# Weight parts of whole projections beside each other, element by element, in one tile

## The chip, the cores and the metric

One core of one Trainium2 chip runs the kernel. The metric is device microseconds of one execution. The engines are TensorE (PE; its weight loads are listed as PEld), VectorE (DVE), ScalarE (ACT), GpSimd (POOL) and the queue of SyncE (SP).

## What is computed

A decoder of two layers over 512 tokens of width 1024 in float32: a gated-DeltaNet layer with six heads, then a layer of sliding-window attention with twelve heads. Both also attend to 256 memory tokens and have a SwiGLU of width 2816.

```python
for layer in range(DEPTH):
    h = rms_norm(x, ln_mix[layer])
    mkv = mem_n @ w_mem_kv[layer]
    ...
        mix_out, mem_q = gated_deltanet_mixer(h, gdn_w_in[a], ...)   # layer 0
    ...
        proj = h @ swa_w_q[bl]                                       # layer 1
        mix_out = sliding_window_attention(q, shared_k, shared_v, swa_sinks[bl])
    mem_o = memory_attention(mem_q, mem_k, mem_v)
    x = x + concatenate([mix_out, mem_o]) @ w_out[layer]
    x = x + swiglu(rms_norm(x, ln_ffn[layer]), w_gate_up[layer], w_down[layer])
    if layer == N_A_LAYERS - 1:
        kv = rms_norm(x, ln_kv) @ w_kv
return rms_norm(x, ln_final)
```

## The kernel before

Activations are kept transposed: 128 features on the partitions, the 512 tokens along the free dimension, eight such tiles for the width of 1024. A projection computes 128 output features for all tokens: for each of eight slices of 128 input features the weights are the stationary operand (128 x 128) and the activations stream past (512 columns).

Exactness comes from two parts. A float32 value is split into a high part, rounded to the type float32r by a copy on ScalarE (L140), and a low part, value minus high, by a subtraction on VectorE (L153). `split` does this for weights and activations. `mm3` then issues three matmuls (L146) for one slice: high weights with high activations, high weights with low activations, low weights with high activations. Each has its own weight load.

`weight` brings one weight tile (128 x up to 1024) by DMA into `wraw` and splits it into `whi` and `wlo`. These have three buffers each, so that splits run up to two projections ahead of TensorE; a buffer is filled again only when its last reader is done. Raw tiles have two buffers. Projections that call `weight` so, without tiles of their own: the GDN input (`win`, 26 of them), 14 of the 16 rows of the two output projections, the queries (8), the shared keys and values (2), the memory keys of layer 1 (2, with only 256 columns streaming), the first gates and ups of each half of the feed-forward (12) and the down projections (two tiles a row, of 768 and 640). Two output rows of the attention layer have the tiles `oh` and `ol`; the last row of the last down projection has tiles named `T`, and it and the row before it stream 256 columns at a time.

The other gates and ups go through `quarters`, which computes two projections with seven products of quarters instead of eight. Its matmuls stream 256 columns and write banks named `g`. Their weights lie in a ring (`ring`): six places for pairs of 512-wide parts, cut out of the three `whi` and `wlo` buffers, hence their width of D + P; the places begin `shift[0]` = P - 8 = 120 columns into the tile. In the memory values (`product` in `mem_and_norm`) the roles are turned: there the split weights stream and the memory tokens are stationary. The first projections of the kernel (`first`) fill three tile pairs piece by piece as the data arrive.

The order of work on each engine is that of the program, with some order added by hand (`nosync`, `after`). Waits between engines follow from the tiles that instructions read and write.

Of the kernel before, what the change touches and what calls it, by code (L numbers as in the profile page):

```python
# [10 lines left out]
F32R = mybir.dt.float32r  # L11
# [7 lines left out]
P = 128  # L19
T = 512  # L20
D = 1024
# [65 lines left out]
class Builder:  # L87
# [91 lines left out]
        self.loaded = self.nc.sync.dma_start(raw, src).ins  # L179
        return raw  # L180

    def weight(self, src, eng=None, raw=None, parts=1, pool=None, tags=("whi", "wlo"), bufs=3, after=None):

        raw = self.load(src) if raw is None else raw
        n = raw.shape[1]
        hi, lo = (self.part(tag, bufs, pool)[:, :n] for tag in tags)
        for i in range(parts):
            s = slice(i * n // parts, (i + 1) * n // parts)
            self.split(raw[:, s], hi[:, s], lo[:, s], eng or self.weng)
            if after is not None:  # L190
                for ins, other in zip((self.copied, self.low), after):
                    self.nosync(ins, other)
        return hi, lo

    def part(self, tag, bufs=3, pool=None):
        return self.t(pool or self.wpool, [P, D if pool else D + P], F32R, tag, bufs)

    def mm3(self, ps, w, k, act, start, stop, more=False):

# [100 lines left out]
    def mem_and_norm(self, ep):  # L300

        nc, a = self.nc, self.a
        e = self.t(ep, [P, KD + 4 * ROUND], F32, "early")
        part = lambda i, n, size: e[:, KD + i * ROUND + n:KD + i * ROUND + n + size]
        mem = [part(k // 2, k % 2 * 2 * ML, ML) for k in range(KD)]
        x = self.t(ep, [P, KD, T], F32, "x")
        mh = self.t(ep, [P, KD, ML], F32R, "mh")
# [5 lines left out]
        raw = [self.load(a["wmk"][j], ep, 4) for j in range(2)]  # L313
# [13 lines left out]
        def product(ps, w, s, k):  # L327
            wh, wl = w[k // 4]
            c = slice((k % 4) * ML, (k % 4 + 1) * ML)
            ins = self.mm(ps, mh[:, k, s], wh[:, c], k == 0, False)  # L330
            self.mm(ps, ml[:, k, s], wh[:, c], False, False)
            self.mm(ps, mh[:, k, s], wl[:, c], False, k == KD - 1)
            return ins

        def first():
            w = [None] * 4
            for n in (2, 0, 1, 3):
                p, bufs = (self.wpool, 3) if n < 3 else (ep, 1)
                w[n] = tuple(self.t(p, [P, D], F32R, t, bufs) for t in ("whi", "wlo"))
            ps = [self.bank("sc" if n == 3 else "pj")[:, :ML] for n in range(4)]  # L340
            cut = lambda n, src, at: self.split(src, *(u[:, at:at + src.shape[1]] for u in w[n]))
            for i in range(4):
                for k in (2 * i, 2 * i + 1):
                    self.split_gain(mem[k], e[:, k:k + 1], mh[:, k, :], ml[:, k, :])
                    if k % 2 == 0:
                        cut(0, part(i, ML, ML), k * P)
                cut(1, part(i, 3 * ML, ML), 2 * i * P)
                cut(2 + i // 2, part(i, 4 * ML, 2 * ML), i % 2 * T)
                for m in range(2):
                    for k in (2 * i, 2 * i + 1):  # L350
                        self.mm3(ps[m], w[m], k, (mh[:, k, :], ml[:, k, :]), k == 0, k == KD - 1)
                for j in range(2):
                    for k in (2 * i, 2 * i + 1):
                        product(ps[2 + j], w[2:], slice(j * P, (j + 1) * P), k)
            return ps
# [21 lines left out]
        def values():  # L377
            w, banks = [], []
            for j in range(2):
                w.append(self.weight(None, nc.vector, raw[2 + j]))  # L380
                yield
            for j in range(2):
                ps = self.bank("pj")[:, :ML]
                banks.append(ps)
                for k in range(KD):
                    ins = product(ps, w, slice(j * P, (j + 1) * P), k)
                    if k + j == 0:
                        self.nosync(ins, self.summed)
            yield
            after = self.copied  # L390
            for j, ps in enumerate(banks):
                vt = self.t(ep, [P, ML], F32, "kt", 4)
                self.copy(vt, ps, scale=mc[:, j:j + 1])
                self.nosync(self.copied, after)
                self.keep(vt, "mv", j)
            yield

        w = self.wab = self.t(ep, [P, KD, P], F32R, "wabs")
# [7 lines left out]
        for i in range(15):  # L406
            self.mm(ps[:, :ML], zero[:, :P], zero, i == 0, i == 14)
        banks = first()
        k1, v1 = keys(), values()
        next(k1)  # L410
        for total in self.sum_of(ep, mem, (4, 4), (self.copied, self.low)):
# [687 lines left out]
    def ffn(self, fp, xp, layer, h, apool, rope=False):  # L1099

        nc, a = self.nc, self.a
# [28 lines left out]
        def ring():  # L1130

            if not places:
                for _ in range(3):
                    two = [self.part(tag) for tag in ("whi", "wlo")]
                    places.extend(tuple(x[:, i * T:(i + 1) * T + P] for x in two) for i in range(2))
            places.append(places.pop(0))
            return [x[:, shift[0]:shift[0] + T] for x in places[-1]]

        def begin(f, up, by, tag, bufs, then):

            o = [self.t(fp, [P, T], F32, tag, bufs) for _ in range(2)]
            steps = self.quarters(fp, [col(f + i, up) for i in range(2)], sums, by, o, ring)
            shift[0] = P - 8
            next(steps)
            while waiting:
                x = waiting.pop()
                self.nosync(self.fn(x, x, AF.Silu), self.held)
            end()
            next(steps)
            open_pairs.append((steps, then, o))  # L1150
            return o
# [15 lines left out]
        for f0 in (0, half):  # L1167
# [22 lines left out]
            for m in range(tail):  # L1190
# [3 lines left out]
                for j, n in ((0, 6), (6, 5)):  # L1194
                    w = down(m, j, n)
# [7 lines left out]
        if tail < KD:  # L1203

            parts = (slice(0, T // 2), slice(T // 2, T))
            own = dict(pool=fp, tags=("T", "T"), bufs=8)
            w = {m: [down(m, j, n, **(own if m == KD - 1 else {})) for j, n in ((0, 6), (6, 5))] for m in range(tail, KD)}
# [5 lines left out]
            for t in parts:  # L1213
                acc = self.acc[:, t]
                for m in range(tail, KD):
                    ps, x = self.bank("pj")[:, :T // 2], self.x[m][:, t]
# [6 lines left out]
                    if seeded:  # L1223
                        x = ps
# [393 lines left out]
```

## Time and profile before

| | |
|---|---|
| median of 3 runs | 1130.63 us (1130.58 to 1131.49) |
| span of the profiled execution | 1129.4 us |
| mean granted TensorE clock | 0.998 |
| busy, share of the span | PE 99%, PEld 87%, DVE 73%, ACT 56%, POOL 6% |

The profiled execution is known by its span, from the first to the last instruction; the runs' times hold a little more around it. In groups of instructions a row gives line, engine, operation, the name of what is written, an arrow, the names of what is read, shapes and a count, then the busy time in all and the mean of one in ns, then the idle time before them and who ended it. Matmuls are pipelined: the mean of one is longer than the time from one start to the next. The chain of work is followed back from the last instruction; in order of time, its pieces give a start, a length and a count.

### The profile page before, as it was taken

What the parts mean: (1) busy time and instruction counts of PE and PEld (TensorE: products, weight loads), DVE (VectorE), ACT (ScalarE), POOL (GpSimd) and SP (SyncE); (2) the same over time, 40 slices, a digit from 0 to 9 for tenths busy, and PEclk for the clock granted to TensorE, in tenths of its full rate; (3) what the DMA queues carried; (4) which work ended last, traced back from release to release, by engine and by line L of the source; (5) the groups of instructions that cost most, each with busy time, mean ns of one, the idle gap of its engine ahead of it and who ended that gap; (6) DMA issues with size and microseconds to landing.
All of it is one profiled execution on the core that took longest, in us unless ns stands there. A gap on an engine that the chain in (4) does not pass through costs nothing.

```text
span 1129.4 us, 19330 instructions
## 1 busy us (share of the span) xinstructions
PE 1119.9 (99%) x7339; PEld 986.1 (87%) x7339; DVE 827.6 (73%) x1553; ACT 634.4 (56%) x1285; POOL 73.2 (6%) x91
## 2 busy tenths in 40 slices
PE   9999999999999999999999999999999999999997
PEld 8888778887899988899988887788999988999986
DVE  7676976577888975588955877839999634889643
ACT  8588664456566632366643555856666422666434
POOL 0000000000021001011000000000111000111001
PEclk9999999999999999999999999999999999999999
DMA  8344252234567536377533321116687533776232
GB/s 314 109 153 149 95 131 86 85 113 145 174 167 195 143 111 169 102 191 195 134 89 102 132 75 38 53 43 180 158 201 185 144 103 105 173 190 156 77 103 87
DMA packets 72401, 151.15 MB, mean 134 GB/s; under 512 B 16956, under 2 KB 18516, under 8 KB 72308
## 3 DMA queue, kind: packets, MB, share of 16 engines
q1 hardware_dynamic: 60884, 129.21, 36.3%
q0 software_dynamic: 11136, 20.45, 11.2%
q8 instruction: 57, 0.93, 0.3%
q14 instruction: 36, 0.29, 0.1%
q10 hardware_dynamic: 288, 0.26, 0.1%
HBM read 142.94 MB, written 6.96 MB: 133 GB/s over the span
## 4 chain that ended last, share of the span: by engine, by line
PE 96%; DVE 2%; ACT 1%; DMA 0%; issue 0%; DVEq 0%; SPq 0%; ACTq 0%
PE pj L146 46%; PE g L146 38%; PE sc L146 6%; PE qk L146 3%; PE pt L146 2%; PE pt L150 1%; PE g L150 1%; DVE big L153 1%; DVE qv L156 0%; DVE btmp L153 0%; DMA early<-in_early 0%; DVE wlo L153 0%; ACT sm L134 0%; DVE T L153 0%; DVE gcr L153 0%
## 5 line engine op out<-in xcount | busy, mean ns | idle before, releaser
L140 ACT ACTIVATE whi<-wraw 128x512 fp32r<-128x512 f32 (+3 forms) x318 | 235.3, 748 | 240.6 <-PE pj L146 164.0
L153 DVE TENSOR_TENSOR wlo<-wraw,whi 128x512 fp32r<-128x512 f32 (+3 forms) x318 | 262.8, 837 | 92.7 <-ACT whi L140 85.2
L146 PE MATMUL pj<-h,whi 128*128 128x512 f32 (+1 forms) x652 | 256.4, 395 | 0.0
L146 PE MATMUL pj<-l,whi 128*128 128x512 f32 (+1 forms) x652 | 254.4, 390 | 0.0
L146 PE MATMUL pj<-h,wlo 128*128 128x512 f32 (+1 forms) x652 | 254.0, 390 | 0.0
L146 PE MATMUL g<-T,whi 128*128 128x256 f32 x1216 | 216.8, 279 | 0.0
L146 PEld LDWEIGHTS g<-T,whi 128*128 128x128 f32 x1216 | 185.1, 188 | 1.3 <-DVE fu L156 1.3
L146 PE MATMUL g<-T,wlo 128*128 128x256 f32 x608 | 169.7, 279 | 0.0
L146 PEld LDWEIGHTS pj<-h,whi 128*128 128x128 f32 x652 | 122.4, 188 | 28.0 <-issue 4.1
L146 PEld LDWEIGHTS pj<-h,wlo 128*128 128x128 f32 x652 | 122.5, 188 | 25.4 <-issue 0.9
L146 PE MATMUL g<-l,whi 128*128 128x256 f32 (+1 forms) x500 | 144.5, 289 | 0.0
L146 PE MATMUL g<-h,whi 128*128 128x256 f32 (+1 forms) x500 | 144.4, 289 | 0.0
L146 PE MATMUL g<-h,wlo 128*128 128x256 f32 (+1 forms) x500 | 144.4, 289 | 0.0
L146 PEld LDWEIGHTS pj<-l,whi 128*128 128x128 f32 x652 | 122.6, 188 | 23.6 <-DVE l L1468 0.3
L146 PEld LDWEIGHTS g<-T,wlo 128*128 128x128 f32 x608 | 114.3, 188 | 0.0
L146 PEld LDWEIGHTS g<-h,whi 128*128 128x128 f32 x500 | 94.0, 188 | 1.9
L146 PEld LDWEIGHTS g<-l,whi 128*128 128x128 f32 x500 | 93.9, 188 | 1.9
L146 PEld LDWEIGHTS g<-h,wlo 128*128 128x128 f32 x500 | 93.9, 188 | 1.8
L1286 POOL DMA_DIRECT2D ws<-in_wgu x38 | 33.5, 881 | 733.0 <-DMA ws<-in_wgu 399.1
L140 ACT ACTIVATE whi<-ws 128x512 fp32r<-128x512 f32 x76 | 48.0, 631 | 42.0 <-PE g L146 35.6
L153 DVE TENSOR_TENSOR wlo<-ws,whi 128x512 fp32r<-128x512 f32 x76 | 52.0, 684 | 5.9 <-ACT whi L140 5.9
L1287 POOL DMA_DIRECT2D ws<-in_wgu x38 | 34.2, 900 | 196.4 <-DVE wlo L153 71.4
(421 smaller groups left out, 1683.2 us busy)
## 6 DMA issues: line engine op xcount, KB each, us to landing
wraw<-in_wgu SPq DMA_DIRECT2D x50, 512.0 KB, 4.4
ws<-in_wgu SPq DMA_DIRECT2D x76, 256.0 KB, 3.4
ws<-in_wgu POOLq DMA_DIRECT2D x76, 256.0 KB, 4.5
wraw<-in_win SPq DMA_DIRECT2D x26, 512.0 KB, 3.6
wraw<-in_wdn SPq DMA_DIRECT2D x32, 384.0 KB, 3.1
wraw<-in_wdn SPq DMA_DIRECT2D x32, 320.0 KB, 2.9
wraw<-in_wgu SPq DMA_DIRECT2D x38, 256.0 KB, 4.0
wraw<-in_wout SPq DMA_DIRECT2D x16, 512.0 KB, 3.6
```

The costliest lines, as they stand in the source:

```text
L140: self.copied = self.nc.scalar.activation(out, in_, AF.Copy, **kw).ins
L146: return self.nc.tensor.matmul(out, lhsT, rhs, start=start, stop=stop, skip_group_check=more).ins
L150: return self.nc.tensor.transpose(out, in_, self.ident[:k, :k]).ins
L153: return eng.tensor_tensor(out=out, in0=a, in1=b, op=op).ins
L1286: nc.gpsimd.dma_start(s1, a22, accum_op=ALU.add)
L1287: nc.gpsimd.dma_start(s3, a21, accum_op=ALU.add)
```

## The change

The high and the low part of a weight tile now come from one tile `whl`, three buffers, of twice the width. For a weight that is loaded as the stationary operand, the high parts are its even elements and the low parts its odd ones (`woven`): neighbouring weights of a part then lie 8 bytes from each other, in the writes of ScalarE, the reads and writes of VectorE and the weight loads. Where the split weights stream (`moving`), where the first tiles are filled and in the ring, the two halves of `whl` are used one behind the other (`apart`), contiguous as before. Weights with tiles of their own (`oh`, `ol`, `T`) stay as they were.

```diff
--- before.py
+++ after.py
@@ -179,11 +179,16 @@
         self.loaded = self.nc.sync.dma_start(raw, src).ins
         return raw
 
-    def weight(self, src, eng=None, raw=None, parts=1, pool=None, tags=("whi", "wlo"), bufs=3, after=None):
+    def weight(self, src, eng=None, raw=None, parts=1, pool=None, tags=None, bufs=3, after=None, moving=False):
 
         raw = self.load(src) if raw is None else raw
         n = raw.shape[1]
-        hi, lo = (self.part(tag, bufs, pool)[:, :n] for tag in tags)
+        if tags is not None:
+            hi, lo = (self.t(pool, [P, D], F32R, tag, bufs)[:, :n] for tag in tags)
+        elif moving:
+            hi, lo = (x[:, :n] for x in self.apart())
+        else:
+            hi, lo = self.woven(self.both()[:, :2 * n])
         for i in range(parts):
             s = slice(i * n // parts, (i + 1) * n // parts)
             self.split(raw[:, s], hi[:, s], lo[:, s], eng or self.weng)
@@ -192,8 +197,18 @@
                     self.nosync(ins, other)
         return hi, lo
 
-    def part(self, tag, bufs=3, pool=None):
-        return self.t(pool or self.wpool, [P, D if pool else D + P], F32R, tag, bufs)
+    def both(self):
+        return self.t(self.wpool, [P, 2 * (D + P)], F32R, "whl", 3)
+
+    def apart(self):
+
+        x = self.both()
+        return x[:, :D + P], x[:, D + P:]
+
+    def woven(self, x):
+
+        y = x.rearrange("p (n i) -> p n i", i=2)
+        return y[:, :, 0], y[:, :, 1]
 
     def mm3(self, ps, w, k, act, start, stop, more=False):
 
@@ -335,8 +350,8 @@
         def first():
             w = [None] * 4
             for n in (2, 0, 1, 3):
-                p, bufs = (self.wpool, 3) if n < 3 else (ep, 1)
-                w[n] = tuple(self.t(p, [P, D], F32R, t, bufs) for t in ("whi", "wlo"))
+                w[n] = (tuple(x[:, :D] for x in self.apart()) if n < 3 else
+                        tuple(self.t(ep, [P, D], F32R, t, 1) for t in ("whi", "wlo")))
             ps = [self.bank("sc" if n == 3 else "pj")[:, :ML] for n in range(4)]
             cut = lambda n, src, at: self.split(src, *(u[:, at:at + src.shape[1]] for u in w[n]))
             for i in range(4):
@@ -377,7 +392,7 @@
         def values():
             w, banks = [], []
             for j in range(2):
-                w.append(self.weight(None, nc.vector, raw[2 + j]))
+                w.append(self.weight(None, nc.vector, raw[2 + j], moving=True))
                 yield
             for j in range(2):
                 ps = self.bank("pj")[:, :ML]
@@ -1131,7 +1146,7 @@
 
             if not places:
                 for _ in range(3):
-                    two = [self.part(tag) for tag in ("whi", "wlo")]
+                    two = self.apart()
                     places.extend(tuple(x[:, i * T:(i + 1) * T + P] for x in two) for i in range(2))
             places.append(places.pop(0))
             return [x[:, shift[0]:shift[0] + T] for x in places[-1]]
```

## The prediction

> **What bounds the kernel now.** I read the page first, its busy shares and its chain, then the chain of waits in order of time, because a busy TensorE here says nothing about its pace.
>
> ```profile
> span 1129.4 us, 19330 instructions
> PE 1119.9 (99%) x7339; PEld 986.1 (87%) x7339; DVE 827.6 (73%) x1553; ACT 634.4 (56%) x1285; POOL 73.2 (6%) x91
> PEclk9999999999999999999999999999999999999999
> PE 96%; DVE 2%; ACT 1%; DMA 0%; issue 0%; DVEq 0%; SPq 0%; ACTq 0%
> ```
>
> 96% of the chain is PE at an unthrottled clock, so a change counts through the pace of the matmuls or not at all. The pace, start to start, is in the chain in order of time: these pieces (start, length, what) are unbroken runs of one kind.
>
> ```profile
> 318.53 86.80 PE g L146 x744
> 407.51 64.65 PE pj L146 x285
> 1113.43 7.30 PE pj L146 x61
> ```
>
> The 285 are 512-column matmuls of the first down projection: 64.65/285 = 226.8 ns each. The 61 at the end are the same kind with 256 columns: 7.30/61 = 119.7 ns. The difference, 107.1 ns for 256 columns, is 0.418 ns a column; 512 columns make 214.3, so 12.5 ns of each matmul are no streaming of columns. The 744 are also 256-column matmuls, those of the ring: 86.80/744 = 116.7, a remainder of 9.6 ns. What differs there is where the weights lie: the ring cuts its places 120 columns into the tile (`shift`). So the remainder depends on addresses by 3.0 ns, which a pure cost of issuing or of switching weights would not.
>
> ```profile
> 1062.18 0.39 PE L146 MATMUL pj<-h,whi 128*128 128x512 f32 x1
> 1062.19 0.19 PEld L146 LDWEIGHTS pj<-l,whi 128*128 128x128 f32 x1
> 1062.41 0.39 PE L146 MATMUL pj<-l,whi 128*128 128x512 f32 x1
> 1062.41 0.19 PEld L146 LDWEIGHTS pj<-h,wlo 128*128 128x128 f32 x1
> ```
>
> Every load runs while the matmul before it streams: both read memory at once, the matmul starting anew every 0.23 us. I take the 12.5 ns as those reads colliding. That is inferred; the 3.0 ns of the ring are its only support.
>
> ```profile
> L146 PEld LDWEIGHTS pj<-l,whi 128*128 128x128 f32 x652 | 122.6, 188 | 23.6 <-DVE l L1468 0.3 <-issue 0.2 <-DVE l L153 0.2
> L146 PEld LDWEIGHTS pt<-pf,vt 128*64 128x64 f32 x168 | 9.0, 137 | 2.1 <-ACT sm L134 1.1 <-issue 1.1
> ```
>
> A load of 128 columns takes 188 ns, one of 64 takes 137: an estimate of 0.80 ns a weight. So today a load moves through memory at 4 bytes per 0.80 ns, 5.0 bytes a ns, and the stream at 4 bytes per 0.418 ns, 9.6: the stream overtakes the load and runs past 512 bytes of its addresses each time.
>
> **The change, part by part.** It adds and removes no instruction and no DMA; it moves tiles and changes steps.
>
> 1. Loads of whole projections step by 8 bytes. From the code, the weights concerned: 26 of the GDN input, 14 of the output (two more have tiles of their own), 8 queries, 2 keys and values, 12 gates and ups are 62 projections of 24 matmuls, 1488; the down projections are 16 + 14 rows of half the width, 33 matmuls each, 990; together 2478 with 512 columns. Another 48 (memory keys) + 66 (row 6 of the last down) = 114 have 256. At 8 bytes per 0.80 ns the load moves at 10.0 bytes a ns against 9.6 of the stream: the two advance side by side, and the distance between them hardly changes during a load (0.4 x 102 ns = 41 bytes instead of 512). If collisions come from one overtaking the other, most go: at most 12.5 ns x 2478 = 31.0 us. The lower end of a gain is what another placing has given, 3.0 x 2478 = 7.4 us. In the other direction, a load now spreads over 1024 bytes instead of 512; if each stretch of memory that it opens costs the stream something, the 12.5 double: +31.0 us. No row shows a load at a step. I take half of the remainder, 6.3 x 2478 = 15.6 us of gain: two streams that keep their distance still collide when they begin in the same place, so all of it is too much; and the ring's 3.0, the nearest row, comes from moving the start alone, where this takes the overtaking away. The 114 add 6.3 x 114 = 0.7, within the half.
>
> 2. The pace of a load itself. At twice the time a weight it would take 128 x 1.6 = 204 ns, with the remainder 217, still under 226.8: hidden behind a 512-column stream. Behind 256 columns it is not: 114 x (217 - 119.7) = 11.1 us. From the other side 0; I take 0 and keep 11.1 for the range.
>
> 3. ScalarE writes high parts, VectorE reads them and writes low parts at the step.
>
> ```profile
> L140 ACT ACTIVATE whi<-wraw 128x1024 fp32r<-128x1024 f32 x66 | 69.3, 1054 | 46.2 <-PE pj L146 42.8 <-DMA wraw<-in_wout 2.6 <-DVE wlo L153 0.4
> L140 ACT ACTIVATE big<-big 96x1024 f32<-96x1024 f32 x1 | 2.0, 2011 | 0.4 <-DVE big L153 0.4
> L153 DVE TENSOR_TENSOR wlo<-wraw,whi 128x1024 fp32r<-128x1024 f32 x66 | 80.0, 1218 | 25.3 <-ACT whi L140 22.7 <-PE pj L146 2.5
> 640.00:745.00 105.00, 104.93 (x671) 81.39 (x670) 79.52 (x245) 71.55 (x210) 0.00 (x0) 1.00 0.20 66
> ```
>
> The only stepped copy of this size is the one that turns `big` (it reads at 128 bytes a step): 2011 ns against 1054 for the same count in a row, 1.9 times. That bounds an 8-byte step from above; the contiguous 1054 bounds it from below. At the upper end a 1024-wide split costs VectorE 1.1 us more. The stage with least room is 640 to 745 us, the attention layer (the columns after the stretch and its length: PE, PEld, DVE, ACT): VectorE 79.5 of 105, and some 16 splits there would make it 79.5 + 17.6 = 97.1, still under 105, but with chains in which PE waits for VectorE; I put up to 8 us on it. I take 0: an 8-byte step is nearer to the contiguous row than to 128 bytes. The cover is the tiles held ready.
>
> 4. One tile in place of two. A buffer comes free with its last matmul, not the high part with the last but one: ScalarE's next split starts 0.23 us later, and VectorE's behind it. Queued behind that split on ScalarE are the next evictions and activations; only the projection two later waits for it. And if a load of a high part must now wait for the low part too, because both lie in one range, that is one split of VectorE, 1.2 us.
>
> ```profile
> ACT whi L140 <- PE pj L146: 164.0, 70, 4.3
>   PEld pj L146: 0.4, 2
> ```
>
> The first row says that ScalarE waited 164 us in 70 waits for PE to free a tile: splits are ready early, held up by three buffers only. The second, of the tile `whi`, says that the loads waited 0.4 us for it in all. Two ready tiles are 2 x 24 x 0.2268 = 10.9 us of cover (6.8 to 8.2 in the down projections), against 0.23 + 1.2. Cost 0; were the cover gone, 126 x 1.4 = 180 us, of which nothing points to more than the start of the kernel, where three tiles are filled as they arrive, and those stay apart.
>
> 5. The ring, the early values and the first tiles keep contiguous halves: no instruction there changes, 0. SBUF's total for the six tiles stays the same.
>
> Sum on the profiled execution: 1129.4 - 15.6 = 1113.8 us span; the runs' median of 1130.63 lies 1.2 above the span, so 1115.0. With less PE time nothing else is late: the next bound, VectorE, has 828 us of work.
>
> **The rivals.**
>
> *The collisions grow (slower).* A load opens twice as much memory; the remainder goes from 12.5 to 25: 1130.6 + 31.0 = 1161.6 us. For it: the stepped copy shows that a wide step can cost 1.9 times. Against: the remainder depends on the start, so it is no plain count of what is opened. It decides as soon as more than the overtaking's share is added, that is from a remainder over 12.5.
>
> *Loads run at half pace (slower).* Part 2: hidden behind 512 columns, 11.1 us behind the 114 short ones, 1141.7. [...]
>
> *Nothing changes.* The 12.5 ns are the price of handing the array over, or of the load however it reads; 1130.6. For it: 226.8 is as steady in a stretch of 285 as a fixed price would be. Against: 9.6 in the ring. [...]
>
> *The splits bind (slower).* Part 3, up to 8 us: 1138.6.
>
> **How the numbers follow.** Fewer collisions 0.52 (own range 1100 to 1123, from 31.0 to 7.4 us); nothing 0.17; more collisions 0.16; half pace 0.10; splits 0.05. Faster 0.52, same 0.17 (within 0.2%, about what a measurement of this kernel can tell from none), slower 0.31. The range goes from 1100 to 1148: nearly all of the first case, no change, half pace and splits, and of the doubling only its small part, up to a remainder of 19.5.
>
> **What would show it.** Right: in the long pj run of the first down projection 285 matmuls take near 62.9 us, 220.5 each, and the ring's 744 still 86.8; the loads stay at 188 ns, splits near 1054 and 1218. Wrong: 226.8 again (the remainder is no collision); about 239 (a load costs by what it opens); loads near 290 ns and the end's 256-column run at 217; a VectorE split near 2.3 us; PE waiting for `whl`. The forecast fails first at the step that takes the remainder for overtaking.

## The result: slower by 1.6%

The changed kernel takes 1149.1 us (median; 1148.0 to 1149.9) against 1130.7: a ratio of 1.016, 95% interval 1.014 to 1.017. The forecast was 1115 us, the other way. The profiled execution has a span of 1148.2 us, 18.8 above that of before.

The page after:

```profile
span 1148.2 us, 19317 instructions
PE 1137.1 (99%) x7339; PEld 1004.7 (88%) x7339; DVE 829.6 (72%) x1553; ACT 643.1 (56%) x1285; POOL 73.1 (6%) x91
PE 96%; DVE 1%; ACT 1%; DMA 1%; issue 0%; SPq 0%; DVEq 0%; ACTq 0%
```

PE has 17.2 of the 18.8 us more as busy time, with the same number of its instructions, and the chain is still PE: most of the time went into the pace. The other 1.6 us PE stood idle; they are looked at below. The chain in order of time after (start, length, what):

```profile
277.96 16.80 PE pj L146 x72
323.21 87.63 PE g L146 x744
413.11 67.14 PE pj L146 x285
480.25 102.25 PE g L146 x852
903.87 66.50 PE pj L146 x285
970.36 103.12 PE g L146 x852
1132.34 7.31 PE pj L146 x61
```

and two rows of the chain before that answer to them:

```profile
274.49 16.32 PE pj L146 x72
472.16 102.05 PE g L146 x852
```

512-column matmuls went from 16.32/72 = 226.7 ns to 16.80/72 = 233.3; in the long down run 67.14/285 = 235.6, in the second layer's 66.50/285 = 233.3. 6.67 ns on 2478 matmuls are 16.5 us. The ring, whose instructions are unchanged, gave 0.8 us in each run of 744 (the second layer's is 87.63 as well). Each run of 852 opens with 24 matmuls of 512 columns, whose 0.16 us are among the 16.5; with these taken off, the ring gave nothing in the first and 0.9 us in the second. That is 2.6 us for the ring and 19.1 in all (the first long down run paid 0.6 on top). It is more than the 17.2 of busy time, because the short runs between waits were above 226.7 before and take less than their share (nine matmuls of the attention layer in 2.08 us before, 231 ns each, and in 2.10 after). The 256-column run at the end is as long as before (7.30).

The idle 1.6 us lie mostly near the end, where the chain of before is unbroken PE and the chain after has two long pieces that are not PE:

```profile
1119.59 4.64 DMA wraw<-in_wdn
1124.26 5.53 ACT T L140 x13
```

The last raw tile of the down projection comes late, and with it the splits into `T`. The profiled execution is the longest of the four of this kernel. The longest of the ten of one_tile (below) has the same two pieces, 4.73 and 5.53 us, and apart_at64 has neither, so this is no part of the pace; how often it happens no run here shows.

The splits and loads, by shape:

```profile
L140 ACT ACTIVATE whl<-wraw 128x1024 fp32r<-128x1024 f32 x66 | 74.9, 1140 | 42.3 <-PE pj L146 34.6 <-DMA wraw<-in_wout 4.1 <-DMA wraw<-in_wkv 2.4
L153 DVE TENSOR_TENSOR whl<-wraw,whl 128x1024 fp32r<-128x1024 f32 x66 | 80.4, 1220 | 29.1 <-ACT whl L140 28.8
L146 PEld LDWEIGHTS pj<-l,whl 128*128 128x128 f32 x652 | 126.6, 194 | 23.5 <-issue 0.5 <-DVE l L1483 0.3 <-DVE l L153 0.2
```

ScalarE's writes at a step take 1140 ns instead of 1054, VectorE's 1220 instead of 1218, a load 194 instead of 188.

### The profile page after: what moved, and what is told of

The parts are those of the page before. It is cut to its first block, busy times and chain, and to the rows that moved or that the text cites. A ratio compares the mean times of both kernels' runs of the same rounds, so it can differ in the third digit from the quotient of the medians.

```text
span 1148.2 us, 19317 instructions
## 1 busy us (share of the span) xinstructions
PE 1137.1 (99%) x7339; PEld 1004.7 (88%) x7339; DVE 829.6 (72%) x1553; ACT 643.1 (56%) x1285; POOL 73.1 (6%) x91
## 4 chain that ended last, share of the span: by engine, by line
PE 96%; DVE 1%; ACT 1%; DMA 1%; issue 0%; SPq 0%; DVEq 0%; ACTq 0%
PE pj L146 46%; PE g L146 38%; PE sc L146 6%; PE qk L146 3%; PE pt L146 2%; PE pt L150 1%; PE g L150 1%; ACT T L140 0%; DMA early<-in_early 0%; DMA wraw<-in_wdn 0%; ACT sm L134 0%; DVE btmp L153 0%; DVE big L153 0%; DVE whl L153 0%; DVE qv L156 0%
## 5 line engine op out<-in xcount | busy, mean ns | idle before, releaser
L146 PE MATMUL pj<-h,whl 128*128 128x512 f32 (+1 forms) x1304 | 429.2, 397 | 0.0
L140 ACT ACTIVATE whl<-wraw 128x512 fp32r<-128x512 f32 (+3 forms) x318 | 244.6, 777 | 249.8 <-PE pj L146 158.5
L153 DVE TENSOR_TENSOR whl<-wraw,whl 128x512 fp32r<-128x512 f32 (+3 forms) x318 | 263.4, 838 | 110.7 <-ACT whl L140 105.7
L146 PEld LDWEIGHTS pj<-h,whl 128*128 128x128 f32 x1304 | 251.4, 194 | 52.8 <-issue 4.7
L146 PE MATMUL pj<-l,whl 128*128 128x512 f32 (+1 forms) x652 | 257.1, 395 | 0.0
L146 PE MATMUL g<-T,whl 128*128 128x256 f32 x1824 | 227.7, 280 | 0.0
L146 PEld LDWEIGHTS g<-T,whl 128*128 128x128 f32 x1824 | 219.8, 188 | 1.5 <-DVE fu L156 1.5
L146 PE MATMUL g<-h,whl 128*128 128x256 f32 (+1 forms) x1000 | 201.6, 290 | 0.0
L146 PEld LDWEIGHTS g<-h,whl 128*128 128x128 f32 x1000 | 162.1, 188 | 3.7
L146 PE MATMUL g<-l,whl 128*128 128x256 f32 (+1 forms) x500 | 144.9, 290 | 0.0
```

Of the source, the lines that this page charges most:

```text
L140: self.copied = self.nc.scalar.activation(out, in_, AF.Copy, **kw).ins
L146: return self.nc.tensor.matmul(out, lhsT, rhs, start=start, stop=stop, skip_group_check=more).ins
L153: return eng.tensor_tensor(out=out, in0=a, in1=b, op=op).ins
```

## Experiments

Theories at the start: **A**, a load costs the stream by the stretches of memory it opens, wherever they lie; **B**, stream and load advance side by side and collide because they begin in the same place; **C**, the joining of two tiles costs. Later runs added **D** (the distance between weights and activations counts), **E** (the place of the weights by itself) and **F** (the time from start to start settles on steps of 6.67 ns).

**one_tile**: only the joining is left.

```diff
-            hi, lo = self.woven(self.both()[:, :2 * n])
+            hi, lo = (x[:, :n] for x in self.apart())
```

> The changed kernel, but every weight's two parts lie one behind the other in the one tile, so that all loads are contiguous; only the joining of two tiles to one is left of the change. If the 8-byte step is what costs (theories A and B below): the 512-column matmuls of the long down run are back at 226.7 ns, loads at 188 ns, 1130 to 1132 us. If the joining costs (a buffer comes free later, other addresses; theory C): 233 ns a matmul or waits for whl, 1140 us or more.

Measured 1131.1 us, ratio 1.0001 (0.9992 to 1.0011); the long runs of the chain are as before to within 0.03 us. C falls: at this place in the tile, the loss comes with the step.

The step is also in the writes of ScalarE and VectorE, which run beside the matmuls. A stretch of the changed kernel in which both stand still (start and end, length, then PE, PEld, DVE, ACT) shows that these are not what is paid:

```profile
967.50:969.90 2.40, 2.40 (x12) 2.00 (x11) 0.00 (x0) 0.00 (x0) 0.00 (x0) 1.00 0.33 109
967.64 0.39 PE L146 MATMUL pj<-l,whl 128*128 128x512 f32 x1
...
969.74 0.39 PE L146 MATMUL pj<-l,whl 128*128 128x512 f32 x1
```

Nine starts in 2.10 us are 233 ns each there too.

**woven_at8, woven_at120, apart_at120**: the place of the parts in the tile, with the step and without.

```diff
-            hi, lo = self.woven(self.both()[:, :2 * n])
+            hi, lo = self.woven(self.both()[:, 8:8 + 2 * n])       # woven_at8; 120 in woven_at120
+            hi, lo = (x[:, 120:120 + n] for x in self.apart())     # apart_at120
```

> The changed kernel with its woven parts beginning 8 elements (32 bytes) into the tile, 8-byte step kept. Theory A: 233 ns, 1149 us. Theory B: a pace of its own, different from that at 0 and at 120 elements by more than 1 ns, on either side.

> The changed kernel with its woven parts beginning 120 elements (480 bytes) into the tile, 8-byte step kept. [...] Theory B (stream and load advance side by side and collide because they begin at the same place of memory's period): another place changes the pace by several ns, to 220 to 227 ns, 1116 to 1131 us.

> Contiguous parts in one tile, beginning 120 columns into it, as the ring's do. Theory A: 226.7 ns, 1131 us, since as many stretches are opened. Theory B, and the reading that the ring's lower remainder comes from its place: 226.7 falls by some 3 ns, 1123 us.

Measured 1144.4 us (ratio 1.012, 1.011 to 1.014), 1145.4 (1.013, 1.011 to 1.014) and 1145.6 (1.013, 1.011 to 1.014). The run of 285 of the first down projection, in the chain of one_tile, woven_at8, woven_at120 and apart_at120, in this order:

```profile
407.56 64.62 PE pj L146 x285
```

```profile
411.30 66.15 PE pj L146 x285
```

```profile
411.94 66.51 PE pj L146 x285
```

```profile
411.04 66.50 PE pj L146 x285
```

226.7, 232.1, 233.4 and 233.3 ns. The last is the surprise: contiguous loads, moved by 480 bytes, pay as much as the 8-byte step. Each spreads over 512 bytes, as in one_tile, and by the expectation opens as many stretches there; so A cannot be the account of it. Of B, half came true: the place changes the pace of stepped loads (232.1 at 32 bytes, over 1 ns from the others), but at 480 bytes they were to fall to 227 or less, and they stayed at 233.4. Both theories were wrong about apart_at120.

**pad8**: the kernel before, with `self.t(cp, [P, 8], F32, "pad")` ahead of the constants.

> The kernel before with a pad of 32 bytes ahead of its constants. Weights and the activations h both move by 32 bytes, so stream and load keep their distance; the activations ac8 to ac10 lie at the other end of the memory and stay, so their distance to the weights becomes 32 bytes. Theory D (what counts is the distance between stream and load, modulo some period): matmuls on h stay near 226.7 ns, those on ac8 to ac10 go to 230 to 234; some 1133 us. Theory E (what counts is where the load lies by itself): all of them go to 230 to 234 ns, 1140 us or more.

The timeline of pad8 around the change from one kind of activations to the other:

```profile
416.34 0.39 PE L146 MATMUL pj<-l,whi 128*128 128x512 f32 x1
...
421.33 0.39 PE L146 MATMUL pj<-h,wlo 128*128 128x512 f32 x1
...
421.79 0.40 PE L146 MATMUL pj<-ac8l,whi 128*128 128x512 f32 x1
...
423.19 0.40 PE L146 MATMUL pj<-ac10l,whi 128*128 128x512 f32 x1
```

and the same matmuls on ac8 to ac10 in the kernel before:

```profile
419.87 0.39 PE L146 MATMUL pj<-ac8l,whi 128*128 128x512 f32 x1
...
421.23 0.39 PE L146 MATMUL pj<-ac10l,whi 128*128 128x512 f32 x1
```

In pad8, 22 starts on h from 416.34 to 421.33 are 226.8 ns each, and six on ac8 to ac10 from 421.79 to 423.19 are 233 ns each; before, the same six took 1.36 us, 226.7 ns. Weights moved by the same 32 bytes in both; only where the activations did not move along did the pace change. So matmul by matmul D holds and E falls. The time, 1140.2 us (ratio 1.008, 1.005 to 1.011), lies above the 1133 that D expected, because the ring's pace rose too: 88.55 us for its 744 and 104.00 for the 852, 7.4 us in its four runs. That there, too, some distances changed and others did not is argued from the layout and not shown.

**apart_at64, apart_at16**: the line of apart_at120 with 64 and with 16.

> Contiguous parts in one tile, beginning 64 columns (256 bytes) into it. If the period of the distance is 256 bytes or less, 226.7 ns and 1131 us as at 0; if it is 512 bytes, a pace of its own, 230 to 234 ns and 1140 to 1146 us.

> Contiguous parts in one tile, beginning 16 columns (64 bytes) into it. If the period of the distance between stream and load is 64 bytes: 226.7 ns, 1131 us, as at 0 and at 256 bytes. If it is 128 or 256: 230 to 234 ns, 1140 us or more.

Measured 1131.0 us (1.0004, 0.9993 to 1.0016) and 1146.4 (1.014, 1.012 to 1.016). At 256 bytes the run of 285 takes 64.64 us, at 64 bytes 66.49. So 256 bytes are a period or a whole number of them, 64 are not; 128 was not tried with contiguous loads of 512 columns.

**half_load**: are the 12.5 ns reads of the load at all?

```diff
-        self.mm(ps, wh[:, s], al, False, False, more)
+        r = slice(k * P, k * P + P // 2)
+        self.mm(ps[:P // 2], wh[:, r], al, False, False, more)     # likewise the others but first and last
```

> The kernel before, with 64 of 128 weight columns loaded in every matmul of a projection but the first and the last of its sum (half of the outputs miss those parts). If the 12.5 ns are collisions of the load's reads with the stream: half as many reads, 6 ns less, 220.0 to 220.5 ns. If they belong to the handing over of the array or to the matmul: 226.7 ns. Loads go from 188 to 137 ns in both.

Its loads by shape, and its run of 285:

```profile
L146 PEld LDWEIGHTS pj<-l,whi 128*64 128x64 f32 x636 | 85.6, 135 | 52.2 <-DVE l L153 0.7 <-DVE l L1470 0.3 <-issue 0.2
```

```profile
407.79 65.52 PE pj L146 x285
```

A load of half the columns takes 135 ns instead of 188, and the matmuls start 229.9 ns apart, 3 ns more, not 6 less; neither expectation came. The remainder is no sum over a load's reads from which a share can be taken off, and this removes the ground of the prediction. It does not show that load and stream leave each other alone: the runs on the distance show that they do not (233.3 ns in apart_at120, 226.7 in one_tile). The one execution took 1135.8 us.

**short504, short496, woven_short504**: fewer columns, without the step and with it.

```diff
-        self.mm(ps, wh[:, s], al, False, False, more)
+        self.mm(ps[:, :504], wh[:, s], al[:, :504], False, False, more)     # likewise the others but first and last
```

> The kernel before, with 504 of 512 columns streamed in every matmul of a projection but the first and the last of its sum (the last 8 tokens miss those parts). Theory F (the time from start to start settles on whole steps of 6.67 ns, as 226.67 = 34 and 233.33 = 35 of them do): 226.7 ns stays, or 220.0, over the long down run. If the pace simply follows the columns: 8 x 0.418 = 3.3 ns less, 223.3 ns.

> The kernel before with 496 of 512 columns streamed in the same matmuls (the last 16 tokens miss those parts). Theory F: one whole step less than at 512, 220.0 ns, while 504 gave 226.7. If 504 was no rounding but a change of address or length that costs: 223 or more.

> The changed kernel with 504 of 512 columns streamed in every matmul of a projection but the first and the last of its sum (the last 8 tokens miss those parts). Theory F1 (the step costs little by itself and only tips the rounding to the next 6.67 ns): 8 columns less tip it back, 226.7 ns. Theory F2 (the step costs most of 6.67 ns by itself): 233.3 ns stays or 230 shows.

The timeline of short504, then a run of 24 in the chain of short496, then the run of 72 in that of woven_short504:

```profile
439.64 0.39 PE L146 MATMUL pj<-l,whi 128*128 128x504 f32 x1
...
441.23 0.39 PE L146 MATMUL pj<-h,wlo 128*128 128x504 f32 x1
```

```profile
293.06 5.29 PE pj L146 x24
```

```profile
274.18 16.37 PE pj L146 x72
```

Seven starts in 1.59 us: 227 ns with 504 columns, the same as with 512 (the whole long down run, 64.82/285, is at 227.4). With 496 columns 5.29/24 = 220.4 (two full-length matmuls among them): one step of 6.67 ns less. Not all of short496 is there: its long down run is at 62.83/285 = 220.5, the second layer's at 63.79/285 = 223.8. So the pace does not simply follow the columns, and F holds in most stretches, but a run can sit between steps. A mean between them closes on whole steps only over a pattern of several matmuls, and with a long enough pattern any mean would; those means are no support for F. And 16 columns at the 0.418 ns of the prediction are 6.7 ns, so a stream that counts in sixteens would also give 504 and 496 as they came; that rival stands, but it does not explain the rise from 226.7 to 233.3 at 512 columns, with the place alone, in apart_at120.

With the 8-byte step, 504 columns take 16.37/72 = 227.4, with two of 24 at full length, against 16.40 in short504: there the step costs nothing. At 512 it tips the pace from 34 steps to 35. The single executions took 1135.1 us (short504), 1121.6 (short496) and 1132.4 (woven_short504). That 8 columns fewer made the kernel 4 us slower and not faster is in part the ring: its first 744 take 87.64 us in short504, and why is open.

**woven_at16, woven_at32, woven_at64**: is there a place where stepped loads settle on 34?

> The changed kernel with its woven parts beginning 16 elements (64 bytes) into the tile. Theory D with a period of 64 bytes: a place equal to 0, so 233.3 ns and 1148 us again. If the 8-byte step by itself costs nothing and a place exists where it settles on 34 steps of 6.67 ns, 226.7 ns and 1131 us could show here; at 0, 8 and 120 elements it did not.

> The changed kernel with its woven parts beginning 32 elements (128 bytes) into the tile. If only the place counts: somewhere within the period the stepped load settles on 34 steps as the contiguous one does, 226.7 ns and 1131 us, and 128 bytes is the place farthest from 0 in a period of 256. If the step itself costs: 230 ns or more here as well, 1139 us or more.

> The changed kernel with its woven parts beginning 64 elements (256 bytes) into the tile. Period of 256 bytes as with contiguous loads: the pace of the changed kernel at 0, 233.3 to 235.6 ns, about 1148 us. A longer period: another pace.

Measured 1139.1 us (1.008, 1.006 to 1.009), 1141.6 (1.009, 1.008 to 1.011) and 1149.1 (1.016, 1.014 to 1.018). Their runs of 285:

```profile
409.69 65.55 PE pj L146 x285
```

```profile
410.50 65.95 PE pj L146 x285
```

```profile
412.76 66.51 PE pj L146 x285
```

230.0, 231.4 and 233.4 ns. At 256 bytes the time of the changed kernel is back, and at 32, 64 and 128 bytes it is another, so 256 bytes are a period for stepped loads as well. Within it, five places gave 230.0 to 235.6; the best is 34.5 steps, a pace that neither expectation of woven_at16 named. The place can take back half of the loss (10 of 18 us, of which 2.6 are the ring, whose 744 are back at 86.80 there), and no place tried takes all.

**ring_16, ring_32**: the kernel before with another place of the ring.

```diff
-            shift[0] = P - 8
+            shift[0] = P - 16      # P - 32 in ring_32
```

> The kernel before with the ring's places beginning 112 columns into the tile instead of 120 (64 bytes from the full period instead of 32). Place decides: the ring's 744 matmuls leave 116.67 ns (17.5 steps); at 113.3 (17 steps) the kernel would gain 3192 x 3.3 = 10.6 us, at 120 (18 steps) lose as much. Nothing else changes.

> The same with the ring's places beginning 96 columns into the tile (128 bytes from the full period): 113.3, 116.7 or 120 ns by place, 1120, 1131 or 1141 us.

```profile
318.46 87.62 PE g L146 x744
```

```profile
318.75 89.29 PE g L146 x744
```

117.8 and 120.0 ns against 116.7; 1134.5 us (1.003, 1.002 to 1.004) and 1141.2 (1.009, 1.007 to 1.010). The second is one of the paces that were named, the first is none. Distance moves 256-column matmuls too, and the kernel before has the best of the places that were tried. No version here that computes everything beats it.

## Why the prediction was wrong, by its steps

**The bound and the count** were right: PE at 96% of the chain, 2478 matmuls on which the change is paid, at one pace but for the first down run (235.6).

**Part 1 failed at its first step**, the 12.5 ns read as collisions of a load's reads with the stream. The 3.0 ns by which the ring's remainder was lower did show that addresses matter, but not that reads are paid one by one, so that fewer or better placed ones would come off the time: half_load loads half the columns and gains nothing, and short504, with fewer columns to stream, gains nothing either. What the runs showed in its place: the time from start to start mostly settles on steps of 6.67 ns, sometimes between two, and which pace it finds depends on the columns (220.4 ns at 496 in short496, 227.4 at 504 in short504), on the distance between weights and activations within 256 bytes (226.7 in one_tile, 233.3 in apart_at16), and on the step of the load. At distance 0 contiguous loads settle on 34 steps (226.67 ns), stepped ones on 35 (233.33), +16.5 us instead of -15.6. The pace argument, 10.0 bytes a ns against 9.6, promised a gain from loads that advance beside the stream, and at none of the six places tried did such loads gain any. That load and stream disturb each other was not the mistake; that the disturbance is an amount that can be taken off was.

The row that should have warned was in hand: 226.7 to 226.8 ns in stretches of 72 and 285, in both layers, is as steady as a fixed pattern. The prediction gave that reading to "nothing changes" and did not ask what a fixed pattern does when it is disturbed.

**The size of the rival.** "The collisions grow" had the sign, not the size (1161.6) nor the mechanism: apart_at120 grows nearly as much (66.50 us for the 285, as in the second layer of the changed kernel), though its loads spread over no more memory than before. The range ended 1 us below the measured time. Its upper end left room for 7.0 ns on each of the 2478, and the 6.67 that came would have fitted, at 1147.1 us; the ring, which part 5 put at nothing, carried the time past it. That the range came so near is luck: its upper end was a share of a doubling that did not happen.

**Part 2** was right: the loads took 6 ns more (194 ns against 188) and did not show behind 256 columns. That it took 0 and not 11.1 us was the author's estimate; no row of before has a load at a step. The run of 61 at the end begins with stepped loads and ends with those of `T`; 26 starts on stepped ones, from 1132.41 to 1135.53 us, are 120.0 ns each, against 119.7 before. A smaller load gained nothing: in half_load it takes 135 ns, and the matmuls start 229.9 ns apart. But where the load begins against the stream does cost, 6.6 ns in apart_at120 (233.3 against 226.7 in one_tile).

**Part 3**: ScalarE's 8% (1140 ns against 1054) and VectorE's 0.2% (1220 against 1218) are near the contiguous end, as taken, and did not show. **Part 4**: one_tile shows it at 0 in the median, within 0.1%; the late last tile in its longest execution is all that speaks for a cost. **Part 5** was wrong by 2.6 us: the ring's instructions did not change, its pace did. In one_tile its 744 take 86.80 us, so the joined tile is not the reason, and in woven_at16 they take 86.80 too, so the step by itself is not either; in the changed kernel the two runs of 852, the same sequence in either layer, differ, 102.25 and 103.12. Why is open.

## What to carry to other kernels

Before a remainder is given a cause, change the amount of the suspected work and see whether it scales; here half the load or 8 columns fewer told more than all the rates worked out from rows. A pace that repeats to a fraction of a ns over hundreds of matmuls may be a pattern that has settled: moving or stepping an operand can then change it for every matmul, here by up to about 9 ns (226.8 to 235.6), with the sign open until a run has shown it. And when a tile's layout changes, look at where both operands of the matmul begin, not only at how they are read.

## What the runs showed of the hardware

- Starts of back-to-back matmuls with 128-column loads mostly settle 33 steps of 6.67 ns apart at 496 columns (220.4 ns in short496), 34 at 504 (227.4 in short504), and 34 (226.7 in the kernel before) or 35 (233.3 in the changed one) at 512; means between steps occur as well (230.0 in woven_at16, 232.1 in woven_at8, and 116.7 with 256 columns in the ring of the kernel before).
- The distance from activations to weights acts, and 256 bytes more bring the pace back: with contiguous loads, and with the kernel before counted as 0, 0 (one_tile) and 256 bytes (apart_at64) give 226.7 and 226.8 ns, 32 (pad8), 64 (apart_at16) and 480 (apart_at120) give 233.
- The same sequence of matmuls can run at two paces within one execution (102.25 and 103.12 us for 852 in the changed kernel).
- Half the weight columns in a load cut the load from 188 to 135 ns and gained nothing (229.9 ns a matmul in half_load, 226.8 before).
- In the changed kernel, loads at an 8-byte step take 194 ns instead of 188; ScalarE writes 1024 elements at that step in 1140 ns instead of 1054.

What makes the step of 6.67 ns, and why the distance selects among its multiples, no run here shows; nor is it excluded that stepped loads settle on 34 steps at a place that was not tried.
